# A hybrid decoder block in float32 on one core: the prologue takes one SiLU and a new order of requests, the DeltaNet preparation moves two-operand work off GpSimd, and the z tiles go ahead of the value tiles

## The chip, the cores and the metric

The kernel runs on one core of a Trainium2 chip. Five engines work beside each other, each through its own instructions in the order in which they were laid down: TensorE (PE) multiplies matrices, VectorE (DVE), ScalarE (ACT) and GpSimd (POOL) work element by element, and SyncE (SP) issues the DMA requests. An instruction waits for the instructions of other engines on which it depends, and everything behind it on its own engine waits with it. The metric is the device time of one execution in microseconds. Before the change it is the median of three runs.

## The reference, cut to what matters

```python
def reference(x, c, ...):
    cond = jax.nn.silu(c)
    for i in range(DEPTH):                     # DEPTH = 1, 512 positions, width 1024
        mod = cond @ w_ada[i] + b_ada[i]
        shift1, scale1, gate1, shift2, scale2, gate2 = jnp.split(mod[:, None, :], 6, axis=-1)
        h = rms_norm(x, norm1_w[i]) * (1.0 + scale1) + shift1
        p = h @ w_in[i]
        qkv_a, z_a, b_a, a_a, p_b, gl_a, gl_b = split_cols(p, IN_SIZES)
        y_a = gated_deltanet(qkv_a, z_a, b_a, a_a, ...)
        y_b = rwkv7_time_mix(p_b, ...)
        merged = jax.nn.sigmoid(gl_a) * (y_a @ w_branch_gdn[i]) + jax.nn.sigmoid(gl_b) * (y_b @ w_branch_rwkv[i])
        x = x + gate1 * (merged @ w_out[i])
        h = rms_norm(x, norm2_w[i]) * (1.0 + scale2) + shift2
        x = x + gate2 * conv_glu(h, w_ffn_in[i], conv_ffn[i], w_ffn_out[i])
    return rms_norm(x, norm_f_w)

def gated_deltanet(qkv, z, b_logit, a_logit, conv_w, a_log, dt_bias, onorm_w):
    qkv = jax.nn.silu(causal_depthwise_conv(qkv, conv_w))
    q, k, v = jnp.split(qkv, 3, axis=-1)
    q = l2_normalize(heads(q)) * (GDN_HEAD_DIM ** -0.5); k = l2_normalize(heads(k))
    o = chunk_gated_delta_rule(q, k, v, g, beta)   # chunks of 64, a triangular solve for each chunk
    return rms_norm(o, onorm_w) * jax.nn.silu(heads(z))
```

## The kernel before

Activations lie transposed: a tile is 128 channels by 512 positions. Every product in float32 is made as three matmuls on rounded halves (`mm3`): weight high part by activation high part, high by low, low by high. A weight tile arrives in a raw buffer (two of them, requested on SP), ACT rounds it (`whi`), and DVE subtracts to get the rest (`wlo`); `split` does both. One output tile of the input projection takes 8 steps along the width, so 24 matmuls of 128x512.

**Prologue.** SP requests `c` and eight tiles of x. The SiLU of `c` is made from an exponential on 128x8 numbers (lines 335 to 338), spread over all partitions by a POOL select (L339), two matmuls with ones (L343) and two copies (L344) into `cond`. Beside it ACT squares the x tiles (L348), DVE adds the squares up (L350), a matmul sums over partitions (L352), and ACT makes `rstd`. Then `first_tiles` runs over the eight steps k for seven output tiles at once, so with seven PSUM banks open: `ada` twice (DVE multiplies a 128x1024 piece of `w_ada` by `cond` and sums it, L202), A1 from it (L366), the normalized tile on DVE and ACT (L305, `hh` L306, `hl` L307), the split of 128x896 raw weights, and 21 matmuls. The low part of the split is on POOL for k above 0.

**DeltaNet preparation.** A queue of output tiles is worked off by a generator; `fill(n)` runs n of its steps wherever the code calls it, `need(label)` runs it until a tile is done. Its order is: two query tiles, two low-rank tiles, four value tiles, then (queued later) key, receptance, value, z and gate tiles. Around it stands: four-tap convolutions (ACT once, L383, DVE three times, L385; one tile has them on ACT and POOL, L414 to L418), SiLU, `l2norm` of four key and four query tiles (square on POOL, L483, matmul L485, logarithm and exponential on ACT, product on DVE), decay factors (`gt` on POOL, L505; `ex` masked on DVE, L512; `ee`, L513; `eg`), and eight chunks of key-by-key and query-by-key products (PE L622, DVE L623 and L627, POOL L624).

**The triangular solves.** `solve` runs once for DeltaNet ("g") and once for RWKV-7 ("r"). It writes the chunk matrices to DRAM (`lsc`, L548), reads them back in another layout (L551), negates (DVE, L552) and masks (POOL, L553), then eliminates in 30 columns of two DVE instructions each (L559, L561), copies (ACT, L565), goes through DRAM again (`tsc`, `usc`), and ends with small matmuls (L582, L592). After it the scan over eight chunks begins (L182); its first matmuls and the L582 of the second solve are used as marks below.

**Where z goes.** A z tile is copied from PSUM by ACT and written to DRAM (`zsc`, by `spill`, L395 and L396). It is read back (L835) after the second solve has begun, and its SiLU gates the DeltaNet output, which eight `w_bg` tiles then project.

A build step lays each engine's instructions down in a fixed order that it derives from the code order and from estimates of its own; so what stands ahead of what on an engine is read from the listings below.

Of the kernel before, what the change touches and what calls it, by code (L numbers as in the profile page):

```python
# [15 lines left out]
F32 = mybir.dt.float32  # L16
# [39 lines left out]
def body(ctx, tc, io, out, tap=lambda name, ap: None):  # L56
# [143 lines left out]
    def ada(j, w):  # L200
        sp.dma_start(w, io["w_ada"][j])
        i = dve.tensor_tensor_reduce(out=w, in0=w, in1=cond, scale=1.0, scalar=col("b_ada", j), op0=ALU.mult,  # L202
                                 op1=ALU.add, accum_out=mod[:, j:j + 1])
        if last["norm"] is not None:
            tc.add_manual_dep(i.ins, last["norm"].ins.name, after, reason="place")
# [103 lines left out]

    def first_tiles(src, count, banks, xs_, ready, side, cut=False, behind=()):  # L310
        for k in range(KT):
            ready(k)
            raw = raw_tile()
            sp.dma_start(raw[:, :128 * count].rearrange("p (n j) -> p n j", n=count),
                         src[0:count].rearrange("n p j -> p n j")[:, :, k * 128:(k + 1) * 128])
            hi = wp.tile([128, 1024], F32R, name="whi", tag="whi", bufs=2)
            lo = wp.tile([128, 1024], F32R, name="wlo", tag="wlo", bufs=2)
            split(hi[:, :128 * count], lo[:, :128 * count], raw[:, :128 * count], side if k else dve, () if k else behind)
            if k == 0 and cut:

# [15 lines left out]
    dve.tensor_scalar(sc_, sc_, 1.0, None, op0=ALU.add)
    dve.reciprocal(sc_, sc_)
    dve.tensor_tensor(sc_, sc_, cc, op=ALU.mult)
    pool.affine_select(out=diag.rearrange("p (k t) -> p k t", k=KT), in_=sc_.unsqueeze(2).broadcast_to([128, KT, 128]),  # L339
                       pattern=[[0, KT], [-1, 128]], base=0, channel_multiplier=1, compare_op=ALU.is_equal, fill=0.0)  # L340
# [19 lines left out]
    made = []  # L360

    def first_h(k):
        w = slot((2, 3, 8, 9, 12)[k]) if k < 5 else slot2((0, 2, 1)[k - 5])
        ada(8 + k, w[:, 0:D])
        ada(k, w[:, D:2 * D])
        dve.scalar_tensor_tensor(A1[:, k:k + 1], mod[:, 8 + k:9 + k], 1.0, col("norm1", k),  # L366
                                 op0=ALU.add, op1=ALU.mult)
# [41 lines left out]

    def gkq(a, j, side=False):  # L410
        def f(p):
            acc, w = tmp("sg" if side else "acc"), col("conv_gdn", 4 * (4 * (1 - a) + j), 4)
            if side:
                act.activation(acc, p, AF.Copy, scale=w[:, 3:4])  # L414
                for i in range(1, 4):
                    t = tmp("sp")
                    act.activation(t[:, :T - i], p[:, :T - i], AF.Copy, scale=w[:, 3 - i:4 - i])
                    pool.tensor_tensor(acc[:, i:], acc[:, i:], t[:, :T - i], op=ALU.add)  # L418
            else:
                conv(acc, p, w, 4)  # L420
# [82 lines left out]
    for b in range(4):  # L503
        gt = tmp("acc").rearrange("p (c h t) -> p c h t", c=2, h=4)
        pool.tensor_tensor(gt, gl[:, 2 * b:2 * b + 2, :].unsqueeze(3).broadcast_to([128, 2, 4, C]),  # L505
                           tri_le.unsqueeze(1).unsqueeze(1).broadcast_to([128, 2, 4, C]), op=ALU.mult)
        gtf = gt.rearrange("p c h t -> p (c h t)")
        p = pa()
        pe.matmul(p, tri_gt, gtf, start=True, stop=True)
        ex = tmp("sg").rearrange("p (c h t) -> p c h t", c=2, h=4)  # L510
        fn(ex, p.rearrange("p (c h t) -> p c h t", c=2, h=4), AF.Exp)
        dve.tensor_tensor(ex, ex, mask2[:, 1, :].unsqueeze(1).unsqueeze(1).broadcast_to([128, 2, 4, C]), op=ALU.mult)  # L512
        dve.tensor_tensor(ee[:, 2 * b:2 * b + 2], ex,  # L513
                          beta[:, 2 * b:2 * b + 2, :].unsqueeze(3).broadcast_to([128, 2, 4, C]), op=ALU.mult)
# [101 lines left out]
    ke, qe = kq[:, 0], kq[:, 1]  # L616
    qs = [qe, ct4(gs[:, 2048:4096])]
    for c in range(NC):
        tc_ = slice(c * C, (c + 1) * C)
# [3 lines left out]
        dve.tensor_tensor(ginv[:, c], p[:, :, 0], ee[:, c], op=ALU.mult)  # L623
        pool.tensor_tensor(qs[1][hs(1), :, tc_], qe[hs(1), :, tc_], eg[hs(1), :, tc_], op=ALU.mult)  # L624
        for e in range(2):
# [22 lines left out]
    zsc = dr.tile([4, 128, T], F32, name="zsc")  # L648
    ysc = dr.tile([KT, 128, T], F32, name="ysc")
# [431 lines left out]
def _arrays(inputs):  # L1081
# [35 lines left out]
    for e in range(2):  # L1117
# [42 lines left out]
```

## Time and profile before

| what | value |
|---|---|
| median of 3 runs | 943.73 us (942.07 to 944.73) |
| the profiled execution's own time | 943.86 us |
| span of its trace | 942.2 us |
| mean granted TensorE clock | 0.970 |
| busy: PE / DVE / ACT / POOL | 887.0 / 548.0 / 413.5 / 150.0 us |
| instructions on POOL | 126 |
| DMA read from HBM | 110.14 MB |

The busy time of PE counts each matmul from its start to its modelled end, and matmuls overlap, so a busy PE can still be a slow one. What a stage costs is read from the starts of its instructions. A row of the timeline gives start, duration, engine, line, operation, output and inputs, the count of merged instructions, and in brackets the idle time of that engine ahead of it with what ended it.

### The profile page before, as it was taken

What the parts mean: (1) busy time and instruction counts of PE and PEld (TensorE: products, weight loads), DVE (VectorE), ACT (ScalarE), POOL (GpSimd) and SP (SyncE); (2) the same over time, 40 slices, a digit from 0 to 9 for tenths busy, and PEclk for the clock granted to TensorE, in tenths of its full rate; (3) what the DMA queues carried; (4) which work ended last, traced back from release to release, by engine and by line L of the source; (5) the groups of instructions that cost most, each with busy time, mean ns of one, the idle gap of its engine ahead of it and who ended that gap; (6) DMA issues with size and microseconds to landing.
All of it is one profiled execution on the core that took longest, in us unless ns stands there. A gap on an engine that the chain in (4) does not pass through costs nothing.

```text
span 942.2 us, 13945 instructions
## 1 busy us (share of the span) xinstructions
PE 887.0 (94%) x5463; PEld 690.9 (73%) x5463; DVE 548.0 (58%) x865; ACT 413.5 (44%) x663; POOL 150.0 (16%) x126
## 2 busy tenths in 40 slices
PE   5989889989989998899999999999999999999996
PEld 3666566876666776777667788888888888888885
DVE  7988988934976684245568537464544544322233
ACT  5247535355537658323465425343333333332231
POOL 2334630001542100011232230000000000010112
PEclk7999989989999999799999999999999999999998
DMA  9741232473234577444567543332232233533322
GB/s 322 261 151 46 67 101 68 144 170 102 58 90 112 197 232 202 142 146 153 186 200 256 181 139 91 106 106 96 90 103 99 89 105 97 173 101 100 96 89 90
DMA packets 81696, 126.26 MB, mean 134 GB/s; under 512 B 26237, under 2 KB 43005, under 8 KB 81566
## 3 DMA queue, kind: packets, MB, share of 16 engines
q1 hardware_dynamic: 81630, 125.36, 42.4%
q8 instruction: 43, 0.70, 0.3%
q14 instruction: 23, 0.19, 0.1%
HBM read 110.14 MB, written 14.68 MB: 132 GB/s over the span
## 4 chain that ended last, share of the span: by engine, by line
PE 70%; DVE 14%; ACT 7%; DMA 3%; issue 3%; POOL 2%; SPq 0%; DVEq 0%; ACTq 0%; POOLq 0%
PE ps_mm L187 19%; PE ps_mm L191 19%; PE ps_mm L190 19%; PE ps_pc L182 3%; DVE wlo L149 2%; ACT whi L146 1%; DVE slot L202 1%; ACT slot L607 1%; DMA wada<-in_w_ada 1%; DVE slotd L202 1%; DVE wada L211 1%; PE ps_pa L592 1%; ACT tmp_rs L94 1%; PE ps_pc L187 1%; PE ps_pa L622 1%
## 5 line engine op out<-in xcount | busy, mean ns | idle before, releaser
L187 PE MATMUL ps_mm<-hh,whi 128*128 128x512 f32 (+1 forms) x714 | 292.1, 410 | 8.5 <-ACT hh L306 3.5
L191 PE MATMUL ps_mm<-hh,wlo 128*128 128x512 f32 (+1 forms) x714 | 282.5, 396 | 4.7 <-POOL wlo L149 3.5
L190 PE MATMUL ps_mm<-hl,whi 128*128 128x512 f32 (+1 forms) x714 | 282.3, 395 | 1.5 <-DVE hl L307 1.5
L149 DVE TENSOR_TENSOR wlo<-raw,whi 128x1024 fp32r<-128x1024 f32 (+2 forms) x133 | 156.7, 1178 | 169.1 <-ACT whi L146 163.5
L146 ACT CAST whi<-raw 128x1024 fp32r<-128x1024 f32 (+2 forms) x140 | 136.9, 979 | 242.8 <-PE ps_mm L190 190.4
L187 PEld LDWEIGHTS ps_mm<-hh,whi 128*128 128x128 f32 x714 | 136.0, 191 | 47.6 <-issue 9.8
L191 PEld LDWEIGHTS ps_mm<-hh,wlo 128*128 128x128 f32 x714 | 136.6, 191 | 37.9 <-POOL wlo L149 5.2
L190 PEld LDWEIGHTS ps_mm<-hl,whi 128*128 128x128 f32 x714 | 136.7, 191 | 32.1 <-issue 3.6
L191 PE MATMUL ps_mm<-slot,wlo 128*128 128x512 f32 (+1 forms) x154 | 58.5, 380 | 1.7 <-DVE wlo L149 1.7
L187 PE MATMUL ps_mm<-slot,whi 128*128 128x512 f32 (+1 forms) x154 | 58.0, 379 | 0.0
L190 PE MATMUL ps_mm<-slot,whi 128*128 128x512 f32 (+1 forms) x122 | 45.4, 372 | 0.0
L968 POOL COPY tmp_rs<-tmp_sq 128x512 f32<-128x512 f32 x2 | 2.1, 1066 | 268.8 <-ACT tmp_sq L965 268.8
L211 DVE CUSTOM_DVE_ANT_0 wada<-wada,cond,cols 128x512 f32<-128x512 f32 x32 | 25.1, 785 | 26.5 <-DMA wada<-in_w_ada 26.3
L211 DVE CUSTOM_DVE_ANT_0 wada<-wada,cond,half 128x512 f32<-128x512 f32 x32 | 25.2, 787 | 21.7 <-DMA wada<-in_w_ada 21.6
L187 PE MATMUL ps_mm<-slotd,whi 128*128 128x512 f32 (+1 forms) x96 | 36.4, 379 | 0.0
L190 PE MATMUL ps_mm<-slotd,whi 128*128 128x512 f32 (+1 forms) x96 | 36.1, 376 | 0.0
L191 PE MATMUL ps_mm<-slotd,wlo 128*128 128x512 f32 (+1 forms) x96 | 36.1, 376 | 0.0
L970 POOL TENSOR_TENSOR tmp_rs<-tmp_rs,tmp_sq 128x512 f32<-128x512 f32 x12 | 19.5, 1624 | 103.8 <-ACT tmp_sq L965 103.8
L191 PEld LDWEIGHTS ps_mm<-slot,wlo 128*128 128x128 f32 x154 | 29.0, 188 | 9.1 <-DVE wlo L149 4.0
L1035 DVE TENSOR_TENSOR tmp_sg<-tmp_acc,ps_mm 128x512 f32<-128x512 f32 x20 | 13.8, 688 | 35.6 <-PE ps_mm L191 35.5
L385 DVE SCALAR_TENSOR_TENSOR tmp_acc<-ps_mm,cols,tmp_acc 128x511 f32<-128x511 f32 (+2 forms) x44 | 32.8, 745 | 0.7
L187 PEld LDWEIGHTS ps_mm<-slot,whi 128*128 128x128 f32 x154 | 28.9, 188 | 5.8 <-ACT whi L146 0.4
(279 smaller groups left out, 1336.0 us busy)
## 6 DMA issues: line engine op xcount, KB each, us to landing
raw<-in_w_in SPq DMA_DIRECT2D x40, 512.0 KB, 3.5
raw<-in_w_fi SPq DMA_DIRECT2D x37, 512.0 KB, 3.5
wada<-in_w_ada SPq DMA_DIRECT2D x64, 256.0 KB, 3.1
raw<-in_w_fo SPq DMA_DIRECT2D x16, 512.0 KB, 3.5
slot<-in_w_ada SPq DMA_DIRECT2D x10, 512.0 KB, 6.8
slot<-in_xT SPq DMA_DIRECT2D x16, 256.0 KB, 4.1
raw<-in_w_out SPq DMA_DIRECT2D x8, 512.0 KB, 3.7
raw<-in_w_in SPq DMA_DIRECT2D x8, 448.0 KB, 4.5
```

What stands on the lines that cost most here:

```text
L94: i = act.activation(*a, **k)
L146: i = act.copy(hi, src)
L149: j = eng.tensor_tensor(lo, src, hi.bitcast(F32), op=ALU.subtract)
L182: last["step"] = pe.matmul(*a, **k)
L187: i = pe.matmul(p, hi, xh, start=start, stop=False)
L190: pe.matmul(p, hi, xl, start=False, stop=False)
L191: pe.matmul(p, lo, xh, start=False, stop=stop)
L202: i = dve.tensor_tensor_reduce(out=w, in0=w, in1=cond, scale=1.0, scalar=col("b_ada", j), op0=ALU.mult, op1=ALU.add, accum_out=mod[:, j:j ...
L211: i = dve.tensor_tensor_reduce(out=w, in0=w, in1=cond[:, part], scale=1.0, scalar=half[:, j:j + 1] if u else col("b_ada", j), op0=ALU.mult ...
L385: dve.scalar_tensor_tensor(acc[:, i:], p[:, :T - i], w[:, taps - 1 - i:taps - i], acc[:, i:], op0=ALU.mult, op1=ALU.add)
L970: pool.tensor_tensor(sums[0], sums[0], sq, op=ALU.add)
L1035: dve.tensor_tensor(t, accs[j], p, op=ALU.mult)
```

## The change

1. The prologue loads `c` already copied to 128 partitions (512 KB in place of 4 KB, requested behind the fourth x tile) straight into `cond`, and one ACT instruction makes its SiLU, behind a load of the SiLU table; the table for exponentials is loaded after it. Exponential, sum, reciprocal, product, select, the two matmuls and the two copies go.
2. `first_tiles` requests weights ahead: both `w_ada` pieces of steps 0, 1 and 2 and the raw tiles of steps 0 and 1 stand ahead of the first step, and every later step requests the raw tile of the next one and the `w_ada` pieces of the one after that.
3. The low part of the prologue's splits is always on DVE; A1 is made on ACT.
4. In the preparation the odd query tile takes the common convolution on DVE; the squares of `l2norm` go from POOL to ACT; `gt` goes from POOL to DVE; the mask of `ex` goes from DVE to two POOL selects of 64 partitions; the products with `eg` go from POOL to DVE, in larger pieces; two transposing copies (`to_natural`) have all their PSUM copies on ACT.
5. The four z tiles are queued ahead of the four value tiles, and `l2norm` runs two queue steps at each place in place of one.

```diff
-    sp.dma_start(cc, io["c"])
     for k in range(KT):
         sp.dma_start(xT(k), io["xT"][k])
+        if k == 3:
+            sp.dma_start(cond, io["c"])
...
-    def first_tiles(src, count, banks, xs_, ready, side, cut=False, behind=()):
+    def first_tiles(src, count, banks, xs_, ready, load, cut=False, behind=()):
+        raws = []
+
+        def fetch(k):
+            if k < KT:
+                load(k)
+                raws.append(raw_tile())
+                sp.dma_start(raws[k][:, :128 * count].rearrange("p (n j) -> p n j", n=count),
+                             src[0:count].rearrange("n p j -> p n j")[:, :, k * 128:(k + 1) * 128])
+
+        for k in range(2):
+            fetch(k)
         for k in range(KT):
+            if k:
+                fetch(k + 1)
             ready(k)
...
-            split(hi[:, :128 * count], lo[:, :128 * count], raw[:, :128 * count], side if k else dve, () if k else behind)
+            split(hi[:, :128 * count], lo[:, :128 * count], raw[:, :128 * count], dve, () if k else behind)
...
+    table(SILU)
+    fn(cond, cond, AF.Silu)
     table(EXP)
-    fn(sc_, cc, AF.Exp, scale=-1.0)
...
-    for u in range(2):
-        p = pc()
-        pe.matmul(p, one, diag[:, T * u:T * u + T], start=True, stop=True)
-        act.copy(cond[:, T * u:T * u + T], p)
...
+    def load_ada(k):
+        for j in ((0,), (1, 2))[k] if k < 2 else (k + 1,):
+            if j < KT:
...
+                sp.dma_start(w[:, 0:D], io["w_ada"][8 + j])
+                sp.dma_start(w[:, D:2 * D], io["w_ada"][j])
...
-        dve.scalar_tensor_tensor(A1[:, k:k + 1], mod[:, 8 + k:9 + k], 1.0, col("norm1", k),
-                                 op0=ALU.add, op1=ALU.mult)
+        act.activation(A1[:, k:k + 1], mod[:, 8 + k:9 + k], AF.Identity, scale=col("norm1", k), bias=col("norm1", k))
...
+    zsc = dr.tile([4, 128, T], F32, name="zsc")
+    for j in range(4):
+        inproj(T_Z + j, spill(zsc[j]))
     for j in range(4):
         inproj(T_GV + j, lambda p, j=j: conv(gv[:, j], p, col("conv_gdn", 4 * (8 + j), 4), 4))
...
-        pool.tensor_tensor(sq, dst, dst, op=ALU.mult)
+        act.activation(sq, dst, AF.Square)
...
         l2norm(kq[:, 0, j], 1.0)
-        fill(1)
+        fill(2)
         l2norm(kq[:, 1, j], 0.125)
-        fill(1)
+        fill(2)
...
-        pool.tensor_tensor(gt, gl[:, 2 * b:2 * b + 2, :].unsqueeze(3).broadcast_to([128, 2, 4, C]),
+        dve.tensor_tensor(gt, gl[:, 2 * b:2 * b + 2, :].unsqueeze(3).broadcast_to([128, 2, 4, C]),
...
-        dve.tensor_tensor(ex, ex, mask2[:, 1, :].unsqueeze(1).unsqueeze(1).broadcast_to([128, 2, 4, C]), op=ALU.mult)
+        for e in range(2):
+            d = ex[64 * e:64 * e + 64]
+            pool.affine_select(out=d, in_=d, pattern=[[0, 2], [0, 4], [1, C]], base=0, channel_multiplier=-1,
+                               compare_op=ALU.is_ge, fill=0.0)
...
+    dve.tensor_tensor(qs[1][hs(1)], qe[hs(1)], eg[hs(1)], op=ALU.mult)
     for c in range(NC):
...
-        pool.tensor_tensor(qs[1][hs(1), :, tc_], qe[hs(1), :, tc_], eg[hs(1), :, tc_], op=ALU.mult)
...
-    to_natural(kq[:, 0], lambda e, c: gkn[hs(1 - e), c])
+    to_natural(kq[:, 0], lambda e, c: gkn[hs(1 - e), c], True)
+    dve.tensor_tensor(qe[hs(0)], qe[hs(0)], eg[hs(0)], op=ALU.mult)
     for ct in range(4):
-        dve.tensor_tensor(qe[hs(0), ct], qe[hs(0), ct], eg[hs(0), ct], op=ALU.mult)
-        pool.tensor_tensor(kq[:, 0, ct], kq[:, 0, ct], eg[:, ct], op=ALU.mult)
+        dve.tensor_tensor(kq[:, 0, ct], kq[:, 0, ct], eg[:, ct], op=ALU.mult)
...
-    to_natural(gv, lambda e, c: gvn[hs(1 - e), c])
+    to_natural(gv, lambda e, c: gvn[hs(1 - e), c], True)
...
-    for j in range(4):
-        inproj(T_Z + j, spill(zsc[j]))
     for n in range(KT):
         inproj(T_GA + n, spill(asc[n]))
```

Three places show how the instructions move. The first is ACT at the start of the program. `tmp_sq` and `tmp_rs` hold the squares of the x tiles, `slot_75` the first four tiles and `slot_76` the last four. Before:

```order
L88 ACT_TABLE_LOAD
L94 ACTIVATE sc<-cc 128x8
L348 ACTIVATE tmp_rs<-slot_75 128x512
L348 ACTIVATE tmp_sq<-slot_75 128x512 x3
L348 ACTIVATE tmp_sq<-slot_76 128x512 x4
L344 COPY cond<-ps_pc 128x512 x2
L94 ACTIVATE tmp_rs<-ps_pa,kc 128x512
```

And with the change:

```order
L88 ACT_TABLE_LOAD
L348 ACTIVATE tmp_rs<-slot_75 128x512
L348 ACTIVATE tmp_sq<-slot_75 128x512 x3
L94 ACTIVATE cond<-cond 128x1024
L88 ACT_TABLE_LOAD
L348 ACTIVATE tmp_sq<-slot_76 128x512 x4
L376 ACTIVATE A_102<-mod,cols 128x1
L94 ACTIVATE tmp_rs<-ps_pa,kc 128x512
```

The SiLU and a second table load stand between the fourth and the fifth square, ahead of everything that makes `rstd`.

The second place is SP around the write and the reading back of the first solve's matrices (`lsc_g`); `raw` are weight tiles, `wada` pieces of `w_ada` for later. Before:

```order
L157 DMA raw<-in_w_in 128x1024
L210 DMA wada<-in_w_ada 128x512
L548 DMA lsc_g<-slotd_830 32x32x32 x4
L157 DMA raw<-in_w_in 128x1024 x2
L551 DMA slot_943<-lsc_g 128x1024
```

And with the change:

```order
L208 DMA wada<-in_w_ada 128x512 x3
L405 DMA zsc<-tmp_sp 128x512
L556 DMA lsc_g<-slotd_851 32x32x32 x4
L405 DMA zsc<-tmp_sp 128x512 x2
L156 DMA raw<-in_w_in 128x1024
L559 DMA slot_957<-lsc_g 128x1024
L405 DMA zsc<-tmp_sp 128x512
```

Between the write and the reading back there were two weight requests; now there are the writes of the second and third z tile and one weight request.

The third place is SP around the same pair of the second solve (`lsc_r`); `asc` receives a gate tile, `tmp_sg` the z tiles read back. Before:

```order
L548 DMA lsc_r<-slotd_2351 32x32x32 x4
L396 DMA zsc<-tmp_sp 128x512 x2
L157 DMA raw<-in_w_in 128x1024
L551 DMA slot_2555<-lsc_r 128x1024
L396 DMA zsc<-tmp_sp 128x512
L835 DMA tmp_sg<-zsc 128x512 x2
```

And with the change:

```order
L556 DMA lsc_r<-slotd_2469 32x32x32 x4
L405 DMA asc<-tmp_sp 128x512
L840 DMA tmp_sg<-zsc 128x512 x2
L559 DMA slot_2673<-lsc_r 128x1024
L405 DMA asc<-tmp_sp 128x512 x2
L156 DMA raw<-in_w_bg 128x512 x2
```

The two z writes and the weight request ahead of the reading back have become a gate write and the reading back of two z tiles.

More of the change, by code (lines that the diff above doesn't have):

```diff
@@ L108, in body @@
     cons = const.tile([128, NCONS], F32, name="cons")
-    diag = slot2(1)[:, 0:D]
-    sc_ = const.tile([128, KT], F32, name="sc")
-    cc = const.tile([128, KT], F32, name="cc")
+    cond = const.tile([128, D], F32, name="cond")
     one = const.tile([128, 128], F32, name="one")
-    sp.dma_start(cc, io["c"])
     for k in range(KT):
         sp.dma_start(xT(k), io["xT"][k])
+        if k == 3:
+            sp.dma_start(cond, io["c"])
     sp.dma_start(cols, io["cols"])
@@ L200, in ada @@
     def ada(j, w):
-        sp.dma_start(w, io["w_ada"][j])
         i = dve.tensor_tensor_reduce(out=w, in0=w, in1=cond, scale=1.0, scalar=col("b_ada", j), op0=ALU.mult,
@@ L308, in norm_h @@
         return i
-    def first_tiles(src, count, banks, xs_, ready, side, cut=False, behind=()):
+    def first_tiles(src, count, banks, xs_, ready, load, cut=False, behind=()):
[8 more added lines that the diff above has]
+            fetch(k)
         for k in range(KT):
+            if k:
+                fetch(k + 1)
             ready(k)
-            raw = raw_tile()
-            sp.dma_start(raw[:, :128 * count].rearrange("p (n j) -> p n j", n=count),
-                         src[0:count].rearrange("n p j -> p n j")[:, :, k * 128:(k + 1) * 128])
+            raw = raws[k]
             hi = wp.tile([128, 1024], F32R, name="whi", tag="whi", bufs=2)
             lo = wp.tile([128, 1024], F32R, name="wlo", tag="wlo", bufs=2)
-            split(hi[:, :128 * count], lo[:, :128 * count], raw[:, :128 * count], side if k else dve, () if k else behind)
+            split(hi[:, :128 * count], lo[:, :128 * count], raw[:, :128 * count], dve, () if k else behind)
             if k == 0 and cut:
@@ L331, in first_tiles @@
                 mm3(banks[i], (blocks(hi), blocks(lo)), i, xs_[k], k == 0, k == KT - 1)
-    cond = const.tile([128, D], F32, name="cond")
+    table(SILU)
+    fn(cond, cond, AF.Silu)
     table(EXP)
-    fn(sc_, cc, AF.Exp, scale=-1.0)
[L336 to L340, printed above, removed]
-    for u in range(2):
-        p = pc()
-        pe.matmul(p, one, diag[:, T * u:T * u + T], start=True, stop=True)
-        act.copy(cond[:, T * u:T * u + T], p)
     total = tmp("rs")
@@ L360, in body @@
     made = []
+    first_w = []
+    def load_ada(k):
+        for j in ((0,), (1, 2))[k] if k < 2 else (k + 1,):
+            if j < KT:
+                w = slot((2, 3, 8, 9, 12)[j]) if j < 5 else slot2((0, 2, 1)[j - 5])
+                first_w.append(w)
+                sp.dma_start(w[:, 0:D], io["w_ada"][8 + j])
+                sp.dma_start(w[:, D:2 * D], io["w_ada"][j])
     def first_h(k):
-        w = slot((2, 3, 8, 9, 12)[k]) if k < 5 else slot2((0, 2, 1)[k - 5])
+        w = first_w[k]
         ada(8 + k, w[:, 0:D])
         ada(k, w[:, D:2 * D])
-        dve.scalar_tensor_tensor(A1[:, k:k + 1], mod[:, 8 + k:9 + k], 1.0, col("norm1", k),
-                                 op0=ALU.add, op1=ALU.mult)
+        act.activation(A1[:, k:k + 1], mod[:, 8 + k:9 + k], AF.Identity, scale=col("norm1", k), bias=col("norm1", k))
         made.append(norm_h(hh[k], hl[k], xT(k), rstd, A1[:, k:k + 1], mod[:, k:k + 1]))
-    first_tiles(io["w_in"], 7, first_ps, hx, first_h, pool, behind=whole)
+    first_tiles(io["w_in"], 7, first_ps, hx, first_h, load_ada, behind=whole)
     sp.dma_start(cons, io["cons"])
@@ L408, in body, with gkq @@
     pool.memset(wt[64:65], 1.0)
-    def gkq(a, j, side=False):
+    def gkq(a, j):
         def f(p):
[L412 to L420, printed above, removed]
+            acc, w = tmp("acc"), col("conv_gdn", 4 * (4 * (1 - a) + j), 4)
+            conv(acc, p, w, 4)
             fn(kq[:, a, j], acc, AF.Silu)
         return f
-    inproj(T_GQ + 2, gkq(1, 2, True), pa)
+    inproj(T_GQ + 2, gkq(1, 2), pa)
     inproj(T_GQ + 3, gkq(1, 3))
@@ L647, in body @@
     rr_ = ar[:, 1]
-    zsc = dr.tile([4, 128, T], F32, name="zsc")
     ysc = dr.tile([KT, 128, T], F32, name="ysc")
@@ L1008, in second_h @@
                                mod[:, 24 + k:25 + k]))
-    first_tiles(io["w_fi"], 7, ffn_ps, h2, second_h, dve, True)
+    first_tiles(io["w_fi"], 7, ffn_ps, h2, second_h, lambda k: None, True)
     fh, fl, pieces = [], [], []
@@ L1129, in _arrays @@
         "xT": np.ascontiguousarray(f["x"][0].T.reshape(8, 128, T)),
-        "c": percol(f["c"][0]),
+        "c": np.broadcast_to(f["c"], (128, D)),
         "cols": np.concatenate([parts[n] for n in COLS], axis=1),
```

## The prediction

> **What bounds the kernel now.** I read the chain of work that ended last first, then windows of the timeline, and then the timelines of single engines around the places of the change.
>
> ```profile
> PE 70%; DVE 14%; ACT 7%; DMA 3%; issue 3%; POOL 2%; SPq 0%; DVEq 0%; ACTq 0%; POOLq 0%
> 40.00:60.00 20.00, 16.70 (x69) 12.15 (x67) 16.65 (x20) 7.01 (x8) 8.19 (x5) 1.00 0.49 169
> 130.00:140.00 10.00, 6.62 (x20) 4.96 (x19) 8.13 (x11) 2.89 (x4) 1.80 (x2) 0.69 0.41 152
> 590.00:610.00 20.00, 20.00 (x90) 16.57 (x89) 7.37 (x9) 5.97 (x8) 0.00 (x0) 1.00 0.38 118
> ```
>
> In a window row stand, behind its length, the busy time and count of PE, PEld, DVE, ACT and POOL, then the granted clock, the DMA share and GB/s. The chain says that PE sets 70% of the span, DVE 14%; where the 30% lie, the windows say. From 590 to 610 us, 90 matmuls take 20 us: 0.222 us each. I use **0.227** (a tile of 24 is 5.45 us). From 40 to 60 us, in the prologue, there are 69, so PE waits there; from 130 to 140 only 20, at a clock of 0.69. So time can be had in the prologue and around the first solve, and elsewhere only by giving PE less to wait for.
>
> The profiled execution took 943.86 us, its span is 942.2, the median of the runs is 943.73. I work against 943.86; it stands 0.13 over the median, which changes nothing.
>
> **Prologue.**
>
> ```profile
> 5.47 5.47 DVE L350 TENSOR_TENSOR tmp_rs<-tmp_rs,tmp_sq 128x512 f32<-128x512 f32 x7 [2.17 <-ACT tmp_sq L348]
> 4.12 0.63 ACT L348 ACTIVATE tmp_rs<-slot 128x512 f32<-128x512 f32 x1 [1.46 <-DMA slot<-in_xT]
> 16.11 1.22 PE L187 MATMUL ps_mm<-hh,whi 128*128 128x512 f32 x2 [3.04 <-ACT hh L306]
> 309.94 1.28 ACT L88 ACT_TABLE_LOAD   x1
> 311.23 0.59 ACT L395 COPY tmp_sp<-ps_mm 128x512 f32<-128x512 f32 x1
> L146 ACT CAST whi<-raw 128x1024 fp32r<-128x1024 f32 (+2 forms) x140 | 136.9, 979 | 242.8 <-PE ps_mm L190 190.4
> ```
>
> Today seven additions end at 5.47 + 5.47 = 10.94, and the first matmul of `first_tiles` starts at 16.11. With the change ACT does a SiLU of 128x1024 and a table load between the fourth and the fifth square. The SiLU isn't in the trace: the square of 512 columns takes 0.63, two of them 1.26; the casts, most of them of 1024, have a mean of 0.98. So between 0.98 and 1.26, and since the square is also a function, 1.2. The load is 1.28. That is 2.5 us; the copied `c` also comes in the middle of x, half a megabyte. Some of both lies in waits for x, so I count **+2.4**: first matmul at 18.5.
>
> By the Trainium skill, "ScalarE: Activation LUTs", section "What ACT_TABLE_LOAD costs", a switch of the set costs the load and about 1.38 us of draining on top, 2.66 in all; then the first matmul would come at 19.9 by estimate. The rows at 309.94 and 311.23 speak against it: the next instruction follows 1.29 us after the load's start.
>
> ```profile
> L366 DVE SCALAR_TENSOR_TENSOR A<-mod,cols x8: 148/152/2071, 13.9 to 54.3; 128x1 f32<-128x1 f32 x8
> L202 DVE CUSTOM_DVE_ANT_0 slotd<-slotd,cond,cols x6: 1277/2203/3132, 37.8 to 51.2; 128x1024 f32<-128x1024 f32 x6
> L149 POOL TENSOR_TENSOR wlo<-raw,whi x7: 2083/2155/2761, 19.4 to 58.4; 128x896 fp32r<-128x896 f32 x7
> 33.89 1.28 DVE L202 CUSTOM_DVE_ANT_0 slot<-slot,cond,cols 128x1024 f32<-128x1024 f32 x1
> 35.09 0.75 DVE L307 SCALAR_TENSOR_TENSOR hl<-tmp_acc,mod,hh 128x512 fp32r<-128x512 f32 x1
> 15.37 1.09 DVE L149 TENSOR_TENSOR wlo<-raw,whi 128x896 fp32r<-128x896 f32 x1
> 64.96 0.39 PE L187 MATMUL ps_pa<-hh,whi 128*128 128x512 f32 x1
> ```
>
> In a row by line the three durations are least, median and most, in ns. The product of 128x1 takes 0.15 us or 2.07, the `w_ada` piece 1.28 or 3.13: DVE is held while the split of 2.1 us runs on POOL. The change takes that split off POOL, and the 128x1 product off DVE. DVE's period is then, from start to start, some 0.08 under the durations: `norm_h` 0.67 and low part of h 0.67 (both instructions of 0.75), `ada` twice 1.20 (33.89 to 35.09), split 1.01: 4.75 us. PE's is 21 matmuls, 4.77. They are about equal, so 18.5 + 8 x 4.77 = 56.7, and I add 3 for a first step at a low clock and for slips between two equal engines: PE has the seven tiles at **59.5**, against 64.96: 5.5 us earlier. A1 goes to ACT, which has room (7.01 busy of 20). The two matmuls that spread `cond` leave a PE that waits anyway.
>
> **Preparation.** It is bound by chains of DVE, ACT and POOL.
>
> ```profile
> 62.36 0.74 DVE L390 SCALAR_TENSOR_TENSOR sg<-ps_mm,cols,sg 32x511 f32<-32x511 f32 x1 [0.81 <-ACT sg L389]
> 83.02 1.28 ACT L88 ACT_TABLE_LOAD   x1
> 110.27 0.41 DVE L623 TENSOR_TENSOR slotd<-ps_pa,slotd 128x256 f32<-128x256 f32 x1
> 120.90 2.60 SPq L548 DMA_DIRECT2D lsc_g<-slotd  x4
> L512 DVE TENSOR_TENSOR tmp_sg<-tmp_sg,cons x4: 1209/1210/1534, 100.5 to 109.1; 128x512 f32<-128x512 f32 x4
> L513 DVE TENSOR_TENSOR slotd<-tmp_sg,beta x4: 676/875/1204, 102.6 to 110.6; 128x512 f32<-128x512 f32 x4
> L385 DVE SCALAR_TENSOR_TENSOR tmp_acc<-ps_mm,cols,tmp_acc x44: 727/745/750, 63.0 to 808.3; 128x511 f32<-128x511 f32 x21, 128x510 f32<-128x510 f32 x21, 128x509 f32<-128x509 f32 x2
> 304.95 2.99 POOL L816 TENSOR_SCALAR_AFFINE_SELECT slot<-slot 64x2048 f32<-64x2048 f32 x1
> 305.88 3.26 DVE L828 SCALAR_TENSOR_TENSOR slotd<-slotd,cols,tmp_rs 128x512 f32<-128x512 f32 x2
> ```
>
> DVE begins on the convolutions at 59.5 in place of 62.36 (it now makes the last low part itself), and has one more of them, 3 x 0.745 = 2.2: the table load of 83.02 comes at about 82. From there to the first L623 are 27.25 us now. Off: the four masks, 4 x 1.21 = 4.8, and about 3 of stalls by POOL. On: four `gt`, between 0.60 (L513's least, start to start) and 1.53 (L512's most) each, taken as 0.60 since nothing else large is left on POOL: 2.4; one product of 64x2048, at most four times L513's 0.68, so 2.7, and taken as 2.3, since one instruction has one start; and what the selects cost. A select of 64x512 is a fourth of L816's 2.99, so 0.75, eight of them 6.0; beside that row two DVE instructions took 3.26 where 0.75 is usual for one. So the selects cost DVE between 0 and 6 us; in that row the pair lost 1.8 of 2.99, and half of the selects I expect beside PSUM or ACT work: **2**. The squares on ACT (0.63) stay in the same chain at the same place and I cost them at nothing. Sum 27.25 - 7.8 + 6.7 = 26.1: the chunks begin at 108, and the write of `lsc_g` comes at **119**, against 120.90. Right behind it DVE takes POOL's four products with `eg` of 128x512, 2.4 us by the same 0.60, and gives its copies of two transpositions to ACT; DVE waits for PE and ACT there (8.13 busy of 10 in the window from 130, ACT 2.89), so I cost the exchange at nothing; without that cover it is 2.4.
>
> By the Trainium skill, "SBUF — State Buffer", section "SBUF: two separate sides", a DVE instruction with two SBUF operands and a GpSimd one that reads SBUF shut each other out for their whole length. The rows at 304.95 and 305.88 fit that; if it held here for all eight selects, 4 us more would stand in the preparation by estimate, which is half of the second rival below.
>
> **First solve.**
>
> ```profile
> 132.95 3.44 SPq L157 DMA_DIRECT2D raw<-in_w_in  x2
> 135.02 0.77 PE L187 MATMUL ps_mm<-hh,whi 128*128 128x512 f32 x1 [3.38 <-DVE slot L385]
> 136.58 0.33 SPq L551 DMA_DIRECT2D slot<-lsc_g  x1
> 150.36 0.19 DVE L559 TENSOR_TENSOR pr<-slot 128x30 f32<-128x30 f32 x1 [1.16 <-POOL slot L553]
> 189.03 0.19 DVE L561 TENSOR_TENSOR slot<-slot,pr 128x30 f32<-128x30 f32 x1
> 201.53 1.19 PE L582 MATMUL ps_pa<-slot,slotd 32*32 32x32 f32 x62 [1.03 <-DMA slot<-tsc_g]
> 208.66 1.12 PE L182 MATMUL ps_pc<-slot,slotd 64*64 64x64 f32 x16
> ```
>
> Written at 120.90, the matrices are requested back only at 136.58, behind a weight pair at 132.95 that waits for a free raw buffer. In the new order the reading back stands behind the writes of the second and third z tile, whose copies wait for PE: with its inputs there from 59.5 on, PE has these two z tiles done at about 131, so the request goes at 131.6 and the columns begin at 139 (a DMA and the two steps ahead of the columns, without the wait for POOL) in place of 150.36. They took 38.7 us, with other work of DVE between them. Now twelve convolution instructions of the value tiles (9 us) fall among them, of which 4 take the place of splits that move away with the shifted tiles, so I take 42.7: the last column is at 182, 7 us earlier, and the matrices are back at about 194. But PE is no longer the one that waits: up to the solve it has 48 more matmuls, since z (96) came in and two shifted tiles (48) stay behind; 10.9 us. Today's window has room for them (20 matmuls in 10 us where 44 would fit), but the value tiles among them wait for DVE; so I take PE at the solve near 200, 6 behind the matrices, where the old row has 201.53; then 7.1 us of solve and the 48 left over, 10.9: the scan begins at 218, **9.3 later** than 208.66 (call this s), with 96 z matmuls = 21.8 us done ahead. Net up to there: 12.5 won.
>
> **Scan** (208.66 to about 284): the same work on the same PE with value and gate tiles beside it; I cost it at nothing. PE hides it.
>
> **Second solve.**
>
> ```profile
> 300.17 2.68 SPq L548 DMA_DIRECT2D lsc_r<-slotd  x4
> 302.94 9.24 SPq L396 DMA_DIRECT2D zsc<-tmp_sp  x2
> 312.84 0.32 SPq L551 DMA_DIRECT2D slot<-lsc_r  x1
> 321.93 0.18 DVE L559 TENSOR_TENSOR pr<-slot 128x30 f32<-128x30 f32 x1
> 359.78 0.19 DVE L561 TENSOR_TENSOR slot<-slot,pr 128x30 f32<-128x30 f32 x1
> 369.04 0.61 SPq L571 DMA_DIRECT2D slotd<-usc_r  x1
> 376.54 1.19 PE L582 MATMUL ps_pa<-slot,slotd 32*32 32x32 f32 x62
> ```
>
> Today the last column is at 359.78, the last request (L571) at 369.04, and with a landing of some 5 us the matrices are back at about 374; PE comes to them at 376.54: chain and PE are level. In the two orders I count, from the scan to this mark, 264 matmuls of tiles before and 219 now: 45 less, 10.2 us. So PE would come at 376.5 + 9.3 - 10.2 = 375.6, with 96 - 45 = 51 matmuls (11.6 us) of later work done already. The chain has its reading back behind the requests of two z tiles, which wait for the buffers of DVE's L842, by the same pace as today at about 313.6 + s in place of 312.84; the columns follow 9 us later as now, and take some 33 us (37.9 now, less the splits of two tiles and the waits with them), and 14 from there: the matrices are back at 369 + s = 378.3. So the mark is set by the **chain**, 1.8 later than now, with 11.6 us of work done: a gain of **9.8 us**. Behind the mark PE is dense (the 590 row), and nothing gives it back: 943.86 - 9.8 = 934.1.
>
> In general the gain is 19.1 - s where the chain sets the mark, and 21.8 - s where PE does; s holds the prologue and the preparation.
>
> **Rivals.**
> 1. *The second solve doesn't bind*, or the first one's columns start as early as 137 and PE isn't late at the scan: gain 21.8 - s with s = 4, so 926 and below. For it: PE is level with the chain today. Against it: reading z back stands ahead of `lsc_r`.
> 2. *About the same.* The selects hold DVE for all of their 6 us (4 more than counted) and PE, which waits for a free bank behind each value convolution, falls to the clock of the 130 to 140 row, 0.69, after an idle of 3.38 us: 10 us at that clock lose 3 us. s = 9.3 + 4 + 3 = 16.3: 941.1. For it: both rows exist. Against it: z gives PE work that needs no DVE.
> 3. *Slower.* The stretch from 60 to 200 is bound by latency and not by PE: the columns of the first solve, with twelve more convolution instructions and their splits in between, end as late as now, and z is not taken in by waits, so that all 21.8 us of z lie ahead of the scan, while the two shifted tiles still follow: s = 22 to 24. Then z is missing as PE's work behind the scan, where the second chain (22 us from the write to the columns, 33 or more of columns) has no cover: the mark comes at 369 + 24 = 393, 16.5 later than now, against 11.6 of work done: 943.86 + 4.9 = 948.8. It decides from s = 19.1 on. For it: PE had 20 matmuls in 10 us here, for want of inputs and not of work. Against it: z needs no input but h.
> 4. *The change doesn't do what it says*: DVE is as slow in the prologue without POOL, since raw tiles or `w_ada` come late: the 5.5 us go, s = 14.8, and the time is 939.6. It lies within the forecast.
>
> **How the numbers follow.** The forecast with its neighbours (926 to 941, the fourth rival in it) gets 0.60, deeper 0.10, about the same 0.17, slower 0.13. 0.3% of 943.7 is 2.8 us, about what a measurement can tell from no change: 940.9 to 946.6. Faster by more: 0.60 + 0.10 = 0.70; same 0.17; slower 0.13. The range leaves out half of the deeper case and most of the slower one, 0.05 + 0.11: **925 to 946**. It holds the bounds of the select (0 to 6), of `gt` (0.60 to 1.53, 3.7 more for four) and of the SiLU (0.98 to 1.26).
>
> **What would show it.** Right: the first matmul of `first_tiles` near 18.5; L202 and the 128x1 product free of 2 us cases; PE at the end of the seven tiles near 59.5; the request that reads `lsc_g` back near 132, the columns from 139; the scan's first L182 near 218; the `lsc_r` request after 320 and the second mark of L582 near 378 with a wait for DMA ahead of it. Wrong: a scan that begins behind 228 (rival 3); a clock under 0.9 between 120 and 200 (rival 2); a second L582 without a wait ahead (rival 1); prologue steps of over 5.5 us (rival 4).

## The result, and the profile after

| | before | changed |
|---|---|---|
| median of 5 runs | 944.73 us (942.07 to 946.39) | 938.37 us (937.80 to 939.77) |
| ratio, with its 95% interval | | 0.9939 (0.9919 to 0.9958) |
| span of the profiled execution | 942.2 us | 936.4 us |
| mean granted TensorE clock | 0.970 | 0.980 |
| busy: PE / DVE / ACT / POOL | 887.0 / 548.0 / 413.5 / 150.0 us | 878.2 / 532.2 / 424.3 / 107.3 us |

The change makes the kernel 6.4 us faster by the medians (5.5 by the two profiled executions). A gain of 9.8 us was forecast.

The marks of the prediction in the timeline of the changed kernel, behind one row of groups by line and one window (the columns are those of before; lines have moved, so L149 is now L148, L182 L181, L187 L186, L202 L200, L551 L559, L552 L560, L559 L567, L571 L579, L582 L590; the row at 58.90 is the first matmul behind the seven tiles):

```profile
19.01 1.22 PE L186 MATMUL ps_mm<-hh,whi 128*128 128x512 f32 x2 [2.98 <-ACT hh L304]
L200 DVE CUSTOM_DVE_ANT_0 slotd<-slotd,cond,cols x6: 1276/1278/1280, 37.1 to 49.4; 128x1024 f32<-128x1024 f32 x6
40.00:60.00 20.00, 20.00 (x90) 16.57 (x89) 17.64 (x26) 11.11 (x16) 0.52 (x1) 1.00 0.62 199
58.90 0.39 PE L186 MATMUL ps_pa<-hh,whi 128*128 128x512 f32 x1
119.14 0.95 SPq L556 DMA_DIRECT2D lsc_g<-slotd  x2
132.09 0.32 SPq L559 DMA_DIRECT2D slot<-lsc_g  x1
203.15 1.19 PE L590 MATMUL ps_pa<-slot,slotd 32*32 32x32 f32 x62
210.44 1.12 PE L181 MATMUL ps_pc<-slot,slotd 64*64 64x64 f32 x16
231.68 0.68 PE L181 MATMUL ps_pc<-cs,slotd 64*64 64x64 f32 x16
```

The row that the prediction took as its mark of the scan, 208.66 before, comes at 210.44, only 1.8 us later: the 48 matmuls left over, which the prediction put ahead of it, stand behind it. So the scan is measured from here on at a later product of it (231.68), which has ahead of it all the work that the prediction put there. The same product in the timeline before:

```profile
218.81 0.68 PE L182 MATMUL ps_pc<-cs,slotd 64*64 64x64 f32 x16
```

From 40 to 60 us, in the prologue, PE makes 90 matmuls where it made 69: it waits for nothing, and the `w_ada` products all take 1.28 us. The seven tiles are done at 58.90, 6.1 us earlier than before. From there the lead shrinks to 1.8 us at the write of `lsc_g`, and that product of the scan comes 12.9 us later than before, with the 96 z matmuls (21.8 us) done.

Behind the scan something shows that was not there before. Windows of the changed kernel, and the rows that make them:

```profile
300.00:340.00 40.00, 34.15 (x287) 24.13 (x278) 29.76 (x60) 26.61 (x54) 9.02 (x5) 0.92 0.45 126
335.00:340.00 5.00, 5.00 (x13) 3.65 (x12) 4.50 (x14) 1.10 (x2) 0.00 (x0) 0.50 0.57 184
324.75 0.32 SPq L559 DMA_DIRECT2D slot<-lsc_r  x1
330.73 1.04 DVE L560 TENSOR_SCALAR slot<-slot 128x1024 f32<-128x1024 f32 x1 [2.30 <-DMA slot<-lsc_r]
331.68 2.34 DVE L148 TENSOR_TENSOR tmp_sq<-tmp_rs,slot 128x512 fp32r<-128x512 f32 x2
332.42 0.50 PE L189 MATMUL ps_mm<-tmp_sq,whi 128*128 128x512 f32 x1 [2.24 <-DVE tmp_sq L148]
383.48 1.19 PE L590 MATMUL ps_pa<-slot,slotd 32*32 32x32 f32 x62
```

Read from the bottom up: PE waits 2.24 us for a half of the gated DeltaNet output (`tmp_sq`), which DVE makes behind L560, and L560 waits 2.30 us for the matrices read back from `lsc_r`, which SP requested only at 324.75, behind the z reads. PE idles three times there, 0.80 us ahead of 329.68, these 2.24, and 0.67 ahead of 334.07; from 335 to 340 the granted clock is 0.50, with 13 matmuls in the 5 us. The window before, over the same stretch, has PE busy all the time:

```profile
300.00:340.00 40.00, 40.00 (x171) 30.95 (x171) 28.73 (x58) 25.09 (x41) 8.76 (x5) 0.99 0.63 191
```

### The profile page after: what moved, and what is told of

It is laid out like the page before. It is cut to its first block, busy times and chain, and to the rows that moved or that the text cites. A ratio compares the mean times of both kernels' runs of the same rounds, so it can differ in the third digit from the quotient of the medians.

```text
span 936.4 us, 13900 instructions
## 1 busy us (share of the span) xinstructions
PE 878.2 (94%) x5459; PEld 687.0 (73%) x5459; DVE 532.2 (57%) x850; ACT 424.3 (45%) x691; POOL 107.3 (11%) x99
## 4 chain that ended last, share of the span: by engine, by line
PE 70%; DVE 10%; ACT 8%; issue 6%; DMA 3%; POOL 2%; SPq 0%; DVEq 0%; ACTq 0%; POOLq 0%
PE ps_mm L186 19%; PE ps_mm L189 18%; PE ps_mm L190 18%; PE ps_pc L181 3%; DVE wlo L148 2%; ACT slot L615 2%; ACT tmp_rs L94 1%; PE ps_pc L186 1%; PE ps_pc L189 1%; PE ps_pc L190 1%; PE ps_pa L186 1%; ACT whi L145 1%; PE ps_pa L189 1%; PE ps_pa L190 1%; PE ps_pa L600 1%
## 5 line engine op out<-in xcount | busy, mean ns | idle before, releaser
L186 PE MATMUL ps_mm<-hh,whi 128*128 128x512 f32 (+1 forms) x714 | 291.2, 409 | 7.6 <-ACT hh L304 3.4
L148 DVE TENSOR_TENSOR wlo<-raw,whi 128x1024 fp32r<-128x1024 f32 (+2 forms) x140 | 161.1, 1151 | 184.5 <-ACT whi L145 178.2
L186 PEld LDWEIGHTS ps_mm<-hh,whi 128*128 128x128 f32 x714 | 135.4, 190 | 47.0 <-issue 7.0
L186 PE MATMUL ps_mm<-slot,whi 128*128 128x512 f32 (+1 forms) x154 | 59.1, 385 | 2.7 <-ACT hh L145 1.5
L190 PE MATMUL ps_mm<-slot,wlo 128*128 128x512 f32 (+1 forms) x154 | 59.5, 386 | 1.8 <-DVE wlo L148 1.8
L186 PEld LDWEIGHTS ps_mm<-slot,whi 128*128 128x128 f32 x154 | 29.7, 193 | 9.3 <-ACT hh L145 1.9
L186 PE MATMUL ps_mm<-slotd,whi 128*128 128x512 f32 (+1 forms) x96 | 36.4, 380 | 0.0
L94 ACT ACTIVATE tmp_acc<-tmp_acc 128x512 f32<-128x512 f32 x22 | 13.9, 631 | 41.5 <-DVE tmp_acc L394 41.4
```

What stands on the lines that cost most here:

```text
L94: i = act.activation(*a, **k)
L148: j = eng.tensor_tensor(lo, src, hi.bitcast(F32), op=ALU.subtract)
L186: i = pe.matmul(p, hi, xh, start=start, stop=False)
L190: pe.matmul(p, lo, xh, start=False, stop=stop)
```

## The experiments

All kernels compute the whole reference. Ratios are to the kernel before on the same chip, with their 95% intervals; its median was 943.98 to 944.39 us there.

Two theories stood at the start, since the gain of 6.4 us is about the 6.1 by which the seven tiles end earlier. A is the account of the prediction: prologue, preparation and z each give something, and the second solve takes part of it back. B is the rival: the prologue is all.

### The three parts alone

Prologue alone (parts 1 to 3 on the kernel before):

> The kernel before with parts 1 to 3 of the change alone (prologue). Theory A (the gain is made of a shorter prologue and of z matmuls that fill waits, and part of it is lost at the second solve): the seven tiles end 5 to 6 us earlier, at about 59, the preparation and both solves start that much earlier, and 4 to 6 us reach the end: 939 to 941. Theory B (the prologue is the whole gain, the rest of the change is worth nothing): the full 6 us, 938 to 939.

Measured: 936.75 us, ratio 0.9929 (0.9905 to 0.9953). By the median that is more than the whole change gives, though the intervals overlap. The first matmul behind the seven tiles in its timeline:

```profile
59.63 0.39 PE L186 MATMUL ps_pa<-hh,whi 128*128 128x512 f32 x1
```

Preparation alone (part 4):

> The kernel before with part 4 alone (GpSimd work of the preparation moved to DVE and ACT). Theory A: the lsc_g write comes up to 1 us earlier or later than 120.9 (one convolution more on DVE, fewer stalls), since the trace after shows 38.1 us from the table load to the write for 37.9 before: 943 to 945. Theory B: no change, 944 to 945.

Measured: 941.93 us, ratio 0.9975 (0.9949 to 1.0001): a gain by the median, and by itself not clear of noise.

z alone (part 5):

```diff
+    for j in range(4):
+        inproj(T_Z + j, spill(zsc[j]))
     for j in range(4):
         inproj(T_GV + j, ...)
...
-        fill(1)
+        fill(2)
```

> The kernel before with part 5 alone (z ahead of the values, two queue steps at each l2norm). Theory A: about 12 us of z's 21.8 are taken in by waits ahead of the scan, 11.6 us of work is done ahead at the mark of the second solve, and the chain of that solve, whose reading back stands behind the z reads, comes 6 to 12 us later: a gain of 0 to 5 us, 940 to 944. Theory B: no change, 944 to 945. Rival of both (z is not absorbed without the shorter prologue): slower, 946 to 950.

Measured: 947.07 us, ratio 1.0032 (1.0014 to 1.0049): slower, beyond noise. The window of this kernel has the same gap as that of the changed one, in PE's busy time and in what ends the longest wait:

```profile
300.00:340.00 40.00, 34.10 (x351) 24.19 (x349) 25.62 (x45) 28.27 (x59) 9.12 (x5) 0.98 0.40 118
338.55 0.80 PE L190 MATMUL ps_mm<-tmp_sq,whi 128*128 128x512 f32 x1 [3.23 <-DVE tmp_sq L149]
```

Theory A, the prediction's account, falls here in its z part, and theory B (z worth nothing) falls to the other side. From now on theory C: z ahead of the values costs, since z tiles were PE's work while the DeltaNet output is normalized and gated.

### The change less one part

Without part 5:

> The changed kernel with part 5 undone (z behind the values again, one queue step at each l2norm). Theory C (after the first runs: z ahead of the values is a loss, since z tiles were what PE worked on while the DeltaNet output is normalized and gated ahead of the w_bg product, where the changed kernel shows PE idle at 329.7 to 334 and then a clock of 0.50): the ratios of prologue alone and preparation alone multiply, 0.993 x 0.9975 = 0.990, so 934 to 937, faster than the whole change. Rival (z costs only where the prologue is long, and pays behind the short one, as the prediction had it): 940 to 943.

Measured: 935.24 us, ratio 0.9903 (0.9873 to 0.9932). As theory C had it; all six runs (934.86 to 937.02) lie under the five of the changed kernel, and the intervals of the two ratios overlap a little. Its window is filled; the first matmul and the marked product of the scan follow the window:

```profile
300.00:340.00 40.00, 39.98 (x174) 31.30 (x173) 30.30 (x66) 21.71 (x34) 3.19 (x2) 1.00 0.61 203
20.22 1.22 PE L186 MATMUL ps_mm<-hh,whi 128*128 128x512 f32 x2 [2.98 <-ACT hh L304]
214.42 0.68 PE L181 MATMUL ps_pc<-cs,slotd 64*64 64x64 f32 x16
```

PE is busy for 39.98 of 40 us where the changed kernel has 34.15, at a clock of 1.00 where that has 0.92.

Without part 4:

> The changed kernel with part 4 undone (prologue and z order alone). Theory C: 0.993 x 1.003 = 0.996, so 939 to 942: slower than the prologue alone. Rival (z pays behind the short prologue): 932 to 935.

Measured: 939.80 us, ratio 0.9962 (0.9940 to 0.9983), as theory C. So z was added three times, and each time the ratio rose: from 1 to 1.0032, from 0.9929 to 0.9962, from 0.9903 to 0.9939. That is 3.0 to 3.4 us. Only the first of the three is beyond noise by itself; the intervals of the other two pairs overlap, so the sign is well supported and the size only likely. Part 4 lowered the ratio three times, by 0.0023 to 0.0026, about 2.3 us of 944; none of the three is clear of noise, so that part 4 helps is only likely.

One queue step at each `l2norm` in place of two, z still ahead:

```diff
-        fill(2)
+        fill(1)
```

> The changed kernel with one queue step at each l2norm in place of two (z stays ahead of the values). Theory C (what costs is z missing as cover behind the scan, not the pace of the queue in the preparation): 937 to 940, as the whole change. Rival (the two steps crowd the preparation, and they are what costs): 934 to 936.

Measured: 940.35 us, ratio 0.9957 (0.9931 to 0.9982). No better than the change, and not the 934 to 936 of the rival: the place of z costs, not the pace.

### What holds up the second solve

The changed kernel, `lsc_r` requested by GpSimd:

```diff
-        sp.dma_start(lt, lsc)
+        (sp if name == "g" else pool).dma_start(lt, lsc)
```

> The changed kernel, with the reading back of the second solve's matrices (lsc_r) requested by GpSimd in place of SP, so that it no longer stands behind the two z reads. Theory A: the request goes at 315 to 318 in place of 324.75, the columns begin at about 325 in place of 333.9, the second mark (L590) moves from 383.5 to 377 to 379, where PE itself comes, and the time is 932 to 935. Theory B (the second solve's chain doesn't hold the end): 938, as the changed kernel.

Measured: 934.75 us, ratio 0.9893 (0.9865 to 0.9921), 3.6 us under the changed kernel's median. The intervals of the two ratios just touch; all six runs (931.64 to 935.54) lie under the five of the changed kernel (937.80 to 939.77). Its timeline:

```profile
319.79 0.76 POOL L559 DMA_DIRECT2D slot<-lsc_r  x1
329.49 1.03 DVE L560 TENSOR_SCALAR slot<-slot 128x1024 f32<-128x1024 f32 x1
332.38 0.18 DVE L567 TENSOR_TENSOR pr<-slot 128x30 f32<-128x30 f32 x1
332.51 0.50 PE L189 MATMUL ps_mm<-tmp_sq,whi 128*128 128x512 f32 x1 [1.17 <-DVE tmp_sq L148]
379.30 0.88 PE L590 MATMUL ps_pa<-slot,slotd 32*32 32x32 f32 x44
```

The request goes 5 us earlier, L560 no longer waits, PE's wait is 1.17 in place of 2.24, and the second mark comes at 379.30 in place of 383.48. The columns begin only at 332.38 and not at 325 as expected, because DVE comes to L560 behind the gating of the z tiles. So theory A had the size and the wait of L560 right, and the way wrong: it is the gated half behind L560 in DVE's queue that comes sooner. The size fits: in the changed kernel PE idles 3.71 us from 329 to 335 and makes 9 matmuls too few behind it (2.0 us at 0.227 each), here it idles 1.07 and 1.17 and the clock stays at 1.00, which is 3.5 us less.

Gate tiles as cover in place of z:

```diff
-    need(T_Z + 3)
+    need(T_GA + 4)
```

> The changed kernel, with the queue run to the fifth gate tile, in place of to the last z tile (which is done by then), ahead of the z reads and the w_bg product. Theory C: PE has gate tiles where before it had z tiles, the idle times of 329.7 to 334 and the clock of 0.50 behind them go, 4 to 6 us: 932 to 935. Rival (it is only the late reading back that holds, and covered time is lost elsewhere): 937 to 939.

Measured: 951.11 us, ratio 1.0068 (1.0048 to 1.0088): slower than both kernels, and theory C had said faster. Three windows of this kernel:

```profile
330.00:340.00 10.00, 10.00 (x45) 8.29 (x45) 8.29 (x21) 6.12 (x9) 1.26 (x1) 1.00 0.71 240
470.00:510.00 40.00, 29.29 (x96) 14.96 (x95) 22.66 (x35) 22.25 (x37) 14.37 (x10) 0.80 0.40 123
476.60 0.80 PE L174 MATMUL ps_pa<-tmp_sg,ones_r 128*128 128x512 f32 x1 [2.17 <-ACT tmp_sg L145]
```

And the second of them in the changed kernel:

```profile
470.00:510.00 40.00, 37.53 (x139) 24.71 (x138) 30.63 (x42) 25.38 (x43) 14.19 (x10) 1.00 0.53 175
```

The gap at 330 closes as expected. But the gate tiles were themselves the cover of the later stage, where the RWKV output is normalized: from 470 to 510 PE makes 96 matmuls in place of 139, waits five times for ACT, 0.88 to 2.17 us each, and its clock falls to 0.80. Cover taken from there costs more than it gives at 330.

Both edits together:

> The changed kernel with both: gate tiles as cover, and the reading back of lsc_r requested by GpSimd. Theory C, with both losses its own: 929 to 932. Rival (both edits mend the same wait): 933 to 935, as the one alone.

Measured: 951.12 us, ratio 1.0076 (1.0049 to 1.0104). As the cover alone. The second mark of the two timelines, the cover alone first:

```profile
395.21 1.19 PE L590 MATMUL ps_pa<-slot,slotd 32*32 32x32 f32 x62
```

```profile
389.26 1.19 PE L590 MATMUL ps_pa<-slot,slotd 32*32 32x32 f32 x62
```

The mark is 6 us earlier and the end is not, so the theory's numbers fall here. Most of the 6 us are only a different order: between the mark and 420 us, the timeline with both edits has 60 matmuls of projection tiles where that of the cover alone has 40, so some 20 of them (4.5 us) have moved behind the mark.

### The prologue

The prologue alone, the low part of steps 1 to 7 back on GpSimd:

```diff
-            split(hi[...], lo[...], raw[...], dve, ...)
+            split(hi[...], lo[...], raw[...], pool if k and not cut else dve, ...)
```

> The kernel e1_prologue (the prologue of the change alone) with the low part of the splits back on GpSimd for steps 1 to 7. Theory (DVE and GpSimd hold each other up in the prologue, and that is what the 5.5 to 6 us are): the 128x1024 w_ada product and others take 2 to 3 us beside the split again, the seven tiles end at 64 to 67, 942 to 946. Rival (the gain is from the weight requests made ahead and from A1 on ACT): the tiles end near 59 to 60, 937 to 939.

Measured: 945.50 us, ratio 1.0009 (0.9987 to 1.0032): the whole gain of the prologue is gone, with all weight requests made ahead. Rows by line, a window, the first matmul behind the tiles, and two splits with the DVE instruction beside each:

```profile
L200 DVE CUSTOM_DVE_ANT_0 slot<-slot,cond,cols x10: 1270/1277/3135, 13.9 to 36.1; 128x1024 f32<-128x1024 f32 x10
L148 POOL TENSOR_TENSOR wlo<-raw,whi x7: 2124/2471/2491, 24.8 to 59.1; 128x896 fp32r<-128x896 f32 x7
40.00:60.00 20.00, 17.44 (x67) 13.14 (x66) 16.63 (x19) 8.68 (x12) 8.47 (x5) 0.91 0.51 171
67.71 0.39 PE L186 MATMUL ps_pa<-hh,whi 128*128 128x512 f32 x1
24.80 2.17 POOL L148 TENSOR_TENSOR wlo<-raw,whi 128x896 fp32r<-128x896 f32 x1 [12.90 <-ACT whi L145]
24.91 3.13 DVE L200 CUSTOM_DVE_ANT_0 slot<-slot,cond,cols 128x1024 f32<-128x1024 f32 x1
31.27 2.47 POOL L148 TENSOR_TENSOR wlo<-raw,whi 128x896 fp32r<-128x896 f32 x1 [4.29 <-ACT whi L145]
31.72 2.56 DVE L303 SCALAR_TENSOR_TENSOR tmp_acc<-slot,A,tmp_rs 128x512 f32<-128x512 f32 x1
```

There are 67 matmuls again from 40 to 60 us, and the tiles end 8.1 us later than in the prologue alone. One `w_ada` product takes 3.13 us again; beside five other splits it is an instruction of the normalized tile (L303 or L305, 0.75 us alone) that takes 1.69 to 2.59. Together the six lose 10.1 us, while DVE has no idle time from 18.31 to 45.44. The Trainium skill, "SBUF — State Buffer", section "SBUF: two separate sides", says that such a pair of two-operand instructions shuts each other out; this run agrees, 3.13 us in place of 1.28 beside a split of 2.17. Whether the weight requests made ahead are needed as well was not tested alone.

The change without part 5, `c` requested behind the eighth x tile:

```diff
-        if k == 3:
+        if k == KT - 1:
             sp.dma_start(cond, io["c"])
```

> The changed kernel without part 5, with the copied c requested behind the eighth x tile in place of the fourth, so that ACT makes the SiLU and the second table load behind all squares. Theory (SiLU and load stand in the way of the sum of squares, 2.3 us of ACT, and the sum sets the first matmul): the first matmul at about 16.5 in place of 19.0, and 1.5 to 2.5 us reach the end: 932.5 to 934. Rival (c and the first w_ada pieces then come too late, the first step is held by them): 935 to 937, as without the edit.

Measured: 932.28 us, ratio 0.9870 (0.9836 to 0.9903): faster than the changed kernel beyond both intervals, and the lowest median of all kernels here. Its first matmul:

```profile
16.66 1.22 PE L186 MATMUL ps_mm<-hh,whi 128*128 128x512 f32 x2 [3.40 <-ACT hh L304]
```

It comes 2.3 us earlier than in the changed kernel. That the end gains as much over the kernel without part 5 alone (0.9903) is likely and not shown, since those intervals overlap.

The same, with `lsc_r` requested by GpSimd:

> As e13_late_silu, and lsc_r read back by GpSimd. Theory C (the late reading back costs only where PE has no cover; with z behind the values PE reaches the second solve behind the matrices, by some 4 us in e5_no_z): no more than 1 us faster than e13_late_silu. Rival (the reading back is worth its 3 to 4 us in any order): 929 to 931.

Measured: 933.31 us, ratio 0.9888 (0.9856 to 0.9920). No gain by the medians, though its request goes at 299.95 in place of 304.99; all six runs (932.20 to 935.76) lie above the rival's 929 to 931. So the late reading back is worth its 3 to 4 us only in the order that leaves PE without work there.

## Why the prediction was right, and where its sum was not

The time, 938.37 us, lies in the range of 925 to 946, and the change is faster, as forecast. But that range also holds no change at all, and the gain is not made as the sum made it: the prologue and, by the medians, the preparation gave all of it, and the z tiles, the largest credit of the sum, cost some. That the total still came out within 4.3 us of the forecast is in part luck.

**The prologue.** Right, in its mechanism and its size. The first matmul was said for 18.5 and came at 19.01, the seven tiles for 59.5 (56.7 + 3 is 59.7) and came at 58.90. That DVE and GpSimd hold each other up, and that the prologue's gain hangs on it, is shown by the run with the splits back on GpSimd. The load of the second table takes 1.29 us to the next instruction (8.80 to 10.09 in the changed timeline), so the draining that the Trainium skill, "ScalarE: Activation LUTs", section "What ACT_TABLE_LOAD costs", adds is not seen here either.

**The preparation.** The write of `lsc_g` came at 119.14 for 119, by luck: two errors cancel. The large product took 2.29 us (2.3 said), but `gt` up to 1.14 (0.60 said), and DVE waited 2.4 us for the selects in addition; so the chunks began at 110.27 and not at 108. The chunk loop then took 8.9 us where before it took 10.6, without the GpSimd products, which the sum had not counted.

**The first solve.** The places were right: reading back at 132.09 (131.6 said), columns from 140.72 (139). PE came to the solve at 203.15 and not at 200. The left-over 48 matmuls stood behind the first product of the scan and not ahead of it, so s is taken at the later product: not 9.3 but 12.9 us. This s is a term that was mis-sized: "96 z matmuls = 21.8 us done ahead. Net up to there: 12.5 won" measured 21.8 - 12.9 = 8.9, and 6.1 of these are the prologue's.

**The second solve.** The reading back went behind the z reads as said, at 324.75, and the mark came at 383.48 where 378.3 was said. That the chain set the mark is not what the trace shows: the sign named for it was a wait for a DMA ahead of the mark, and PE has none there. It runs without idle time from 374.81 on, and the last request of the matrices had gone 5.6 us before:

```profile
377.86 0.61 SPq L579 DMA_DIRECT2D slotd<-usc_r  x1
```

Such requests took 3.6 us to land (the median of the four), so the matrices were back near 381.5: chain and PE were about level, as before. The late matrices worked another way: they held DVE, DVE then held PE's operands from 329 to 335, and the clock fell behind that; the prediction left this path out. With the measured s the prediction's own formula, 19.1 - s, gives 6.2 us, and 6.4 were measured. That agreement is luck. For z alone the same product of the scan starts at 236.03, so s is 17.2 and the formula gives a gain of 1.9, while its median is 2.8 over.

**The step that failed** is the credit for z. The prediction took z as work that can be done anywhere, and counted 12.5 us won by the scan. Parts 1 to 4 alone give 0.9903 and the whole change 0.9939: z ahead took about 3 us of the gain back. Against the kernel without part 5, counted from each kernel's first matmul, the scan comes 18.5 us later ((231.68 - 19.01) - (214.42 - 20.22)), so waits ahead of it took in only 3.3 of z's 21.8 us. Then the window from 300 to 340 loses 5.8 us of PE's busy time, against that kernel, and 9 more matmuls by the clock.

**The rivals.** The third had this mechanism, cover missing behind the scan, and placed it at the columns; it showed itself earlier, at the gating, and on the kernel with the long prologue it decided the sign, at an s of 17.2 and not from 19.1 on. Its sign, a scan behind 228, did not show: the row named came at 210.44. The second had the selects make DVE wait, 2.4 of its 6 us, but from 120 to 200 no window of 10 us has a clock under 0.90. The first rival's sign, a second mark without a wait ahead, did show, but not its gain, since PE had lost its time before. The fourth did not happen.

## What to carry to other kernels

Independent matmuls on a PE-bound kernel are not free to move: each stretch bound by a chain of other engines needs its share, and a tile moved to an earlier wait is missing at a later one. So price a move by the worst stretch that loses it, and try the parts of a change alone: here parts 1 to 4 without the fifth gave, by the medians, 3 us more than the whole. Where a DMA request stands behind others that wait for an engine, look also at what its late landing holds in that engine's own queue.

## What the runs showed of the hardware that was not expected

- The clock fell without one long wait: after idle times of 0.80, 2.24 and 0.67 us on PE, all between 329 and 335 us, the granted clock from 335 to 340 was 0.50, and 13 matmuls stood there where 22 fit. With waits of 1.07 and 1.17 at the same place (`lsc_r` by GpSimd) the clock from 330 to 340 stayed at 1.00. This is one trace of each; which of the waits decides is not shown.
- A product of 128x1 took 0.39 us on ACT, where DVE took 0.15. That moving it to ACT pays by itself was not tested.
- The first matmul of kernels with the same prologue came between 18.88 and 20.22 us: over a microsecond of the difference of two traces can lie ahead of all work that was changed.
